# Rotary attention scores on one core: the last eight rows of five GpSimd loads sent, four at a time, to DMA engines 14, 15, 0 and 1

## The chip, the cores and the metric

The kernel runs on one core of a Trainium2 chip. The metric is device time in microseconds (us) of one execution; the lower the better. The core has 16 DMA engines, here numbered 0 to 15, which carry every transfer between HBM and SBUF.

## The reference

Queries and keys are rotated (rotary embedding), and then every query position is multiplied with every key position of the same batch and head. All is float32; nothing follows the scores.

```python
batch, seq, heads, dim = 16, 512, 16, 64
q_rot = concat([q1 * cos - q2 * sin, q1 * sin + q2 * cos], axis=-1)   # q1, q2: halves of dim
k_rot = the same of k
scores = einsum('bshd,bthd->bsht', q_rot, k_rot)                      # 16 x 512 x 16 x 512
```

The two inputs hold 33.6 MB each, the scores 268.4 MB.

## The kernel before

**Tiling.** A batch has 512 positions, four to each of the 128 partitions. A load brings one batch of q or k, 2 MB, as 128 rows of 16 KB (`load`). The work goes in 64 steps `i`, four to a batch. A step multiplies the 16 heads of 128 query positions with all 512 keys (`scores`, L205), copies each pair of heads out of PSUM on ScalarE into a stage tile `st` (L212), and stores that tile, 4 MB, as 128 rows of 32 KB (`store`, L192). There are three stage tiles. In the first four steps (batch 0) sixteen 1 MB stores take the place of these (L215).

**What goes ahead of a step.** VectorE rotates the tiles of q for step i+2 and of k for step i+5 (`rope`, L153, L154, L158). TensorE transposes them (L174) through two PSUM banks; the copies out of those banks are VectorE's for q and ScalarE's for k (L189). Within a step VectorE's queue is written out by hand: products of q, the copy of one bank, sum of q, the copy of the second bank, then products and sum of k. Input tiles have two buffers for each of q and k, so a load waits until TensorE has transposed the batch that held its buffer.

**Queues.** The Sync queue (SP) issues the stores and most loads in the program's order. Its transfers are the queue q1 of the profile; ScalarE's are q10, GpSimd's q0.

**The five GpSimd loads.** `RELIEVED` names five loads, numbered x = 0 to 4: q of batch 6, k of 7, q of 11, k of 12, q of 15. These are not issued by SP but by `load_around`. Its main part moves rows 0 to 119 as two 8 KB pieces each; the eight rows that are left go by another transfer. GpSimd's transfers of n rows, n under 16, are meant to take n engines in a row from a cursor, eight rows of the main part to each of 15 engines. The small loads of `move_cursor(n)`, n rows of 16 bytes into a `scratch` tile that nobody reads, are there to move that cursor by n. Engine 4 (`SLOW`) is the one that the main part leaves out: the cursor stands at 5 when the main part is issued, so it takes 5 to 15 and 0 to 3.

The eight rows that are left go in 2 KB pieces. For even x ScalarE issues them (L102, queue q10), and they go to engines 0 to 7. For odd x GpSimd issues them ahead of the main part, with the cursor at 8, to engines 8 to 15.

Of the kernel before, what the change touches and what calls it, by code (L numbers as in the profile page):

```python
# [10 lines left out]
def kernel(  # L11
# [8 lines left out]
    nc = tc.nc  # L20
# [4 lines left out]
    B, S, H, D = q.shape  # L25
    HD = D // 2
    P = 128
    C = S // P
# [46 lines left out]

    RELIEVED = {("q", 6): 0, ("k", 7): 1, ("q", 11): 2, ("k", 12): 3, ("q", 15): 4}
    SLOW = 4
    scratch = const_pool.tile([P, 96], fp32, name="scratch")
    tiny = [0]  # L80

    def move_cursor(n):

        y = tiny[0]
        tiny[0] += 1
        src = bass.AP(q.tensor, 512 * y, [(512, n), (64, 2), (1, 2)])
        nc.gpsimd.dma_start(scratch[:n, 4 * y : 4 * y + 4].rearrange("p (a b) -> p a b", a=2), src)

    def load_around(which, b, t):

        n, E, SMALL = 120, C * H * D, C * H * D // 8
        x = RELIEVED[which, b]
        d = dram[which][b]

        def pieces(queue, lo, hi, F):
            k = E // F
            src = bass.AP(d.tensor, d.offset + lo * E + E - F, [(E, hi - lo), (-F, k), (1, F)])
            v = t[lo:hi].rearrange("p c e -> p (c e)")  # L100
            dst = bass.AP(v.tensor, v.offset + E - F, [v.ap[0], (-F, k), (1, F)])
            queue.dma_start(dst, src)  # L102

        if x == 0:
            nc.gpsimd.inc_swdge_sem([], [], mode="reset_dge_cursor")
        else:

            move_cursor(16 - SLOW)
        if x % 2:
            move_cursor(8)  # L110
            pieces(nc.gpsimd, n, P, SMALL)
        move_cursor(SLOW + 1)
        pieces(nc.gpsimd, 0, n, E // 2)
        if not x % 2:
            pieces(nc.scalar, n, P, SMALL)

    def load(which, b):

        if b >= B:
            return  # L120
        t = in_pool.tile([P, C, H * D], fp32, tag=which + "_in", name=which + "_sb")
        batches[which, b] = t
        if (which, b) in RELIEVED:
            load_around(which, b, t)
        else:
            nc.sync.dma_start(t.rearrange("p c (h d) -> p c h d", h=H), dram[which][b])
# [199 lines left out]
```

## Time and profile before

| | |
|---|---|
| time, three runs | 792.38, 792.46, 793.31 us; median 792.46 us |
| span of the profiled execution | 789.9 us |
| span short of that median | 2.6 us, which lies around the span |
| TensorE busy | 687.7 us, 87% |
| ScalarE busy | 561.2 us, 71% |
| VectorE busy | 543.8 us, 69% |
| GpSimd busy | 11.9 us, 2% |
| moved by DMA | 336.18 MB, mean 426 GB/s |

The profiled execution has no time of its own beside its span; the three runs were made without a profile. The profile is of one execution: each instruction with start, length and what it waited for, each DMA packet with its queue, start, length and size, and for every transfer the times of the 16 semaphore steps by which the 16 engines report it done. The packets do not carry the number of their engine.

### The profile page before, as it was taken

How to read it: one execution, taken by the hardware profiler on the slowest of the kernel's cores; microseconds unless marked ns; L12 is line 12 of the kernel's file. 1: busy time of each engine (PE TensorE's matmuls, PEld its weight loads, DVE VectorE, ACT ScalarE, POOL GpSimd, SP SyncE). 2: the span in 40 equal slices, each digit the busy share in tenths (PEclk: the TensorE clock that was granted, in tenths of full speed). 3: DMA queues.
4: the chain of work that ended last, by engine and by line, in shares of the span. 5: the costliest groups of instructions: out<-in, count | busy, mean ns of one | idle time of the engine just before them, and what ended most of it. 6: DMA issues, size and time to landing. Idle time of an engine off the chain costs nothing.

```text
span 789.9 us, 7753 instructions
## 1 busy us (share of the span) xinstructions
PE 687.7 (87%) x3072; PEld 297.4 (38%) x3072; DVE 543.8 (69%) x516; ACT 561.2 (71%) x647; POOL 11.9 (2%) x24
## 2 busy tenths in 40 slices
PE   4999998989978989798897988989899798899960
PEld 2444443433423434243343433434334343344420
DVE  7999987667855859566676666767678486587400
ACT  3888886866847868486685865877577586588770
POOL 0000000000001000000000000100000000000000
PEclk9999999999998999899899898999899899899995
DMA  9999999999999999999999999999999999999997
GB/s 353 421 426 440 429 431 435 424 434 440 428 427 429 429 425 406 428 431 436 430 431 434 427 431 427 429 432 429 427 437 422 437 433 433 428 431 436 430 431 339
DMA packets 19100, 336.18 MB, mean 426 GB/s; under 512 B 2376, under 2 KB 3656, under 8 KB 4936
## 3 DMA queue, kind: packets, MB, share of 16 engines
q1 hardware_dynamic: 16288, 324.61, 96.1%
q0 software_dynamic: 1872, 10.10, 3.1%
q10 hardware_dynamic: 904, 0.98, 0.4%
q8 instruction: 24, 0.39, 0.2%
q14 instruction: 12, 0.10, 0.0%
HBM read 67.24 MB, written 268.44 MB: 425 GB/s over the span
## 4 chain that ended last, share of the span: by engine, by line
DMA 46%; PE 39%; DVE 7%; ACT 4%; issue 1%; ACTq 0%
DMA out_dram<-st 45%; PE ps L205 29%; PE bank L174 9%; ACT st L212 4%; DVE part L153 2%; DVE early L154 1%; DVE early L158 1%; DMA early<-in_q_dram 1%; DVE k_sb L158 1%; DVE k_sb L154 1%; DVE kT_t L189 0%; DVE q_sb L154 0%; DVE q_sb L158 0%; ACTq L321 0%; DVE qT_t L189 0%
## 5 line engine op out<-in xcount | busy, mean ns | idle before, releaser
L212 ACT COPY st<-ps 128x1024 f32<-128x1024 f32 x512 | 495.0, 1020 | 193.7 <-DMA out_dram<-st 109.1
L205 PE MATMUL ps<-kT_t,qT_t 64*128 64x512 f32 x2048 | 545.6, 650 | 64.3 <-ACT st L212 64.1
L205 PEld LDWEIGHTS ps<-kT_t,qT_t 64*128 64x128 f32 x2048 | 183.3, 196 | 255.3 <-issue 135.4
L189 DVE COPY qT_t<-bank 128x512 f32<-128x512 f32 x118 | 81.5, 690 | 186.5 <-PE bank L174 186.5
L174 PEld LDWEIGHTS bank<-ident,q_sb 128*128 128x128 f32 x480 | 55.4, 151 | 100.5 <-issue 97.6
L174 PE MATMUL bank<-ident,q_sb 128*128 128x128 f32 x480 | 86.8, 308 | 0.4 <-PE ps L205 0.4
L174 PEld LDWEIGHTS bank<-ident,k_sb 128*128 128x128 f32 x480 | 50.3, 140 | 94.6 <-issue 42.3
L174 PE MATMUL bank<-ident,k_sb 128*128 128x128 f32 x480 | 78.6, 287 | 1.2 <-DVE qT_t L189 1.2
L153 DVE TENSOR_TENSOR part<-k_sb,ss_t 128x1024 f32<-128x1024 f32 x60 | 72.9, 1215 | 9.3 <-DMA k_sb<-in_k_dram 9.2
L189 ACT COPY kT_t<-bank 128x512 f32<-128x512 f32 x122 | 72.4, 598 | 6.9 <-PE bank L174 6.9
L154 DVE TENSOR_TENSOR k_sb<-k_sb,cos_t 128x1024 f32<-128x1024 f32 x60 | 73.5, 1225 | 2.0
L158 DVE TENSOR_TENSOR k_sb<-k_sb,part 128x1024 f32<-128x1024 f32 x60 | 73.5, 1225 | 2.1
L154 DVE TENSOR_TENSOR q_sb<-q_sb,cos_t 128x1024 f32<-128x1024 f32 x60 | 73.5, 1225 | 2.1
L153 DVE TENSOR_TENSOR part<-q_sb,ss_t 128x1024 f32<-128x1024 f32 x60 | 73.5, 1224 | 2.0
L158 DVE TENSOR_TENSOR q_sb<-q_sb,part 128x1024 f32<-128x1024 f32 x60 | 72.9, 1215 | 0.0
L174 PE MATMUL bank<-ident,early 128*128 128x128 f32 x64 | 10.5, 316 | 12.2 <-DVE early L158 9.7
L174 PEld LDWEIGHTS bank<-ident,early 128*128 128x128 f32 x64 | 8.3, 161 | 17.3 <-issue 13.9
L153 DVE TENSOR_TENSOR part<-early,ss_t 128x1024 f32<-128x1024 f32 x8 | 9.8, 1222 | 5.7 <-DMA early<-in_k_dram 4.9
L102 POOL DMA_DIRECT2D q_sb<-in_q_dram x3 | 2.3, 754 | 617.4 <-PE bank L174 617.4
L158 DVE TENSOR_TENSOR early<-early,part 128x512 f32<-128x512 f32 x16 | 10.3, 685 | 0.2
L154 DVE TENSOR_TENSOR early<-early,cos_t 128x1024 f32<-128x1024 f32 x8 | 9.8, 1225 | 0.3
L189 ACT COPY qT_t<-bank 128x512 f32<-128x512 f32 x10 | 5.7, 628 | 3.3 <-PE bank L174 3.3
(12 smaller groups left out, 15.9 us busy)
## 6 DMA issues: line engine op xcount, KB each, us to landing
out_dram<-st SPq DMA_DIRECT2D x60, 4096.0 KB, 25.2
k_sb<-in_k_dram SPq DMA_DIRECT2D x13, 2048.0 KB, 27.7
q_sb<-in_q_dram SPq DMA_DIRECT2D x12, 2048.0 KB, 27.6
out_dram<-st SPq DMA_DIRECT2D x16, 1024.0 KB, 14.5
q_sb<-in_q_dram POOLq DMA_DIRECT2D x3, 1920.0 KB, 29.2
k_sb<-in_k_dram POOLq DMA_DIRECT2D x2, 1920.0 KB, 43.2
early<-in_k_dram SPq DMA_DIRECT2D x1, 1536.0 KB
early<-in_q_dram SPq DMA_DIRECT2D x1, 1536.0 KB, 12.4
```

Of the source, the lines that this page charges most:

```text
L102: queue.dma_start(dst, src)
L153: nc.vector.tensor_tensor(pv, xs, ss, op=mult)
L154: nc.vector.tensor_tensor(xc, xc, cs, op=mult)
L158: nc.vector.tensor_tensor(y, y, z, op=add)
L174: nc.tensor.transpose(bank[:, x, :], src, ident)
L189: copy(out=dst, in_=src)
L205: nc.tensor.matmul(out=po, lhsT=lhs[64 * r : 64 * r + 64, :], rhs=rh, start=True, stop=True)
L212: nc.scalar.copy(out=so, in_=si)
```

## The change

All eight left rows of all five loads are now issued by GpSimd, ahead of the main part, as two transfers of four rows each, in 8 KB pieces like the main part's. Before each of the two the cursor is moved to 14, so that each puts one row on the engines 14, 15, 0 and 1. ScalarE's three transfers are gone, and the order of the rows is the same for all x. GpSimd issues 30 transfers where it issued 18: 15 cursor moves in place of 11, 15 transfers of rows in place of 7.

```diff
-    SLOW = 4
+    SLOW, AHEAD = 4, 14
...
-        n, E, SMALL = 120, C * H * D, C * H * D // 8
+        n, E = 120, C * H * D
...
         if x == 0:
             nc.gpsimd.inc_swdge_sem([], [], mode="reset_dge_cursor")
-        else:
-
-            move_cursor(16 - SLOW)
-        if x % 2:
-            move_cursor(8)
-            pieces(nc.gpsimd, n, P, SMALL)
-        move_cursor(SLOW + 1)
+        move_cursor(AHEAD if x == 0 else (AHEAD - SLOW) % 16)
+        pieces(nc.gpsimd, n, n + 4, E // 2)
+        move_cursor(12)
+        pieces(nc.gpsimd, n + 4, P, E // 2)
+        move_cursor((SLOW + 1 - AHEAD - 4) % 16)
         pieces(nc.gpsimd, 0, n, E // 2)
-        if not x % 2:
-            pieces(nc.scalar, n, P, SMALL)
```

GpSimd's order for x = 0 was: cursor 5, main part (and ScalarE's eight rows). It becomes: cursor 14, four rows, cursor 12, four rows, cursor 3, main part. For odd x it was: cursor 12, cursor 8, eight rows, cursor 5, main part; for x = 2 and 4 cursor 12, cursor 5, main part. For x = 1 to 4 it becomes: cursor 10, four rows, cursor 12, four rows, cursor 3, main part. TensorE, VectorE and SP have the same instructions in the same order as before.

## The prediction

> **What bounds the kernel now.** I read the page's queue rows first.
>
> ```profile
> q1 hardware_dynamic: 16288, 324.61, 96.1%
> q0 software_dynamic: 1872, 10.10, 3.1%
> q10 hardware_dynamic: 904, 0.98, 0.4%
> q8 instruction: 24, 0.39, 0.2%
> ```
>
> The last column adds up to 99.8% of 16 engines' span: the DMA engines never rest, and no compute engine is over 87%. So time is packet time, and what a change of engines can bring lies in how evenly the 16 finish. The DMA row of the last 15 us (40 slices of 0.37 us) shows that they don't:
>
> ```profile
> DMA  9299489969969948948896696692492226000000
> ```
>
> The busy share fades from about 782.7 us on. The 16 semaphore steps of the last store, in the trace, give each engine's end: 782.71, 782.87, 783.55 and 783.64 us for four leaders, twelve from 785.8 on, the last 789.02. Their mean is 786.56, so perfect balance would gain 2.46 us (0.31%), and no more.
>
> Next, the waits on transfers and the issues:
>
> ```profile
> ACT st L212 <- DMA out_dram<-st: 109.1, 41, 6.2
> DVE part L153 <- DMA k_sb<-in_k_dram: 9.2, 2, 4.6
> ...
> out_dram<-st SPq DMA_DIRECT2D x60, 4096.0 KB, 25.2
> q_sb<-in_q_dram POOLq DMA_DIRECT2D x3, 1920.0 KB, 29.2
> k_sb<-in_k_dram POOLq DMA_DIRECT2D x2, 1920.0 KB, 43.2
> ```
>
> ScalarE waits for stage tiles, as it should when DMA is the bound; a store takes 25.2 us to land though 8 packets of 1.21 us are 9.7 us of work, so more than one store is queued. But the two k loads of GpSimd are already late: VectorE waits 4.6 us for each.
>
> **Who the leaders are.** A packet starts 3 to 4 ns before the one ahead of it on its engine ends, so the packets can be chained into engines. Around 500 us the leaders' chains on q0 differ as the small transfers do: used engines show a 16-byte packet for a cursor row, others an 8-byte filler. Two leaders show cursor 12 used (4 to 15), cursor 8 unused, four 4 KB packets of the eight rows, cursor 5 unused: they lie in 8 to 15. Two show 12 unused, 8 used, no rows, 5 used: they lie in 0 to 3. One chain with 32 KB packets of 1.24 to 1.26 us, where the others take 1.213, carries no main part: engine 4. None of the 16 KB instruction packets (q8) after 500 us falls on a leader. If the leaders stand side by side, only 14, 15, 0, 1 has two in each group. The packets do not show it outright.
>
> **The change, part by part.** An 8 KB packet takes 309 ns, 0.305 net of the overlap, so a row as two of them 0.61 us. A row as ScalarE's eight 2 KB packets (84 ns) was 0.64 us, and as GpSimd's four of 4 KB (159 ns) 0.62.
> - Engines 14, 15: ten rows more, two less: 6.1 − 1.2 = +4.9 us.
> - Engines 0, 1: ten more, three less: 6.1 − 1.9 = +4.2 us.
> - Engines 2 to 7, the relieved 4 among them: three less, −1.9 us.
> - Engines 8 to 13: two less, −1.2 us.
> - Cursor rows, fillers and semaphore packets: counted transfer by transfer some 28 more packets per engine, at 6 ns net: +0.2 us everywhere.
>
> If 14, 15 are the leaders without ScalarE's rows, they end at 782.87 + 4.9 = 787.8; 0, 1 at 783.64 + 4.2 = 787.8; the last other engine at 789.02 − 1.2 = 787.8 (it is one of 8 to 13; engine 4, 0.1 us ahead of it, gains 1.9). With the small packets 788.0 in place of 789.02: **−1.0 us**. From the span to the run: 792.46 − 1.0 = 791.4 us. ScalarE's three issues (0.72 to 1.29 us) vanish from a queue that waits 109.1 us anyway: nothing; if that cover were gone, 2.7 us at most. GpSimd's twelve more issues at 0.56 to 0.76 us: nothing, its engine is idle for 617 us before three of them; uncovered, they would delay a main part by 2.4 us.
>
> **The wait that the change adds.** On an engine with both queues filled, q0 and q1 take turns packet by packet: in the main part of x = 0 the 8 KB packets of one engine come 1.5 us apart (1.213 + 0.309), and each small transfer needs two turns (its semaphore steps come 2.4 us after those of the one ahead). By the Trainium skill ("DMA: Bandwidth & Descriptors", Queues, rings and completion order) an engine round-robins its queue rows by packet; the trace agrees with the 1.5 us.
>
> From the start of x = 0 to the end of x = 1 there were 17 + 2 + 2 + 5 + 2 + 17 = 45 turns (main, cursors 12 and 8, eight rows, cursor 5, main). There will be 3 + 2 + 3 + 2 + 17 = 27 and 2 + 3 + 2 + 3 + 2 + 17 = 29: 56. The q load has 10 turns more, at 1.2 us: it lands at 257.7 + 12 = 270, and VectorE took it at 268.65, a wait of some 1 us. The k load has 11 more: 293.05 + 13 = 306.
>
> ```profile
> 287.84 0.69 DVE L189 COPY qT_t<-bank 128x512 f32<-128x512 f32 x1 [3.66 <-PE bank L174]
> 293.17 1.22 DVE L153 TENSOR_TENSOR part<-k_sb,ss_t 128x1024 f32<-128x1024 f32 x1 [4.63 <-DMA k_sb<-in_k_dram]
> ...
> 299.35 0.68 DVE L189 COPY qT_t<-bank 128x512 f32<-128x512 f32 x1
> ```
>
> VectorE's wait grows from 4.6 to about 18 us, and the copy of 299.35 stands behind it. TensorE's transposes at 300.70 need that bank, the scores behind them stop, and the stores issued at 305.15, 315.17 and 332.75 us move to about 318, 328 and 338 (10 us a step). They are hidden by what is queued: the leaders finished the transfer ahead of each at 321.7, 331.4 and 341.1. At x = 3 it is closer: stores of 550.84, 560.86 and 577.93 move to 563, 573 and 583, against 564.7, 574.4 and 584.1; since the first packets come about 2 us after an issue (2.3 us to the first semaphore step of a 64 KB load at the start), the leaders may idle up to 1 us. The other twelve come 2 to 6 us later, and the leaders by then carry some 3.6 us more than before, so I take **0**; bounds: 0 and, at 6 us more lateness at both places, +6 us. A gain from it is excluded, as no packet disappears. The q loads (x = 2 and x = 4) land at about 514 and 709 us, and VectorE takes those tiles at 514.1 and 709.2: nothing, or 1 to 2 us of VectorE alone.
>
> **The rivals.**
> - *The leaders are not all 14, 15, 0, 1.* Then an engine that ends between 785.8 and 789.0 gets 4.2 to 4.9 us more, and the end moves to between 790 and 793.9: 793.4 to 797.4 us. For it: the class is shown, not the number. Against it: the two classes, and the instruction packets that pass the leaders by. It decides once one of the four ends after 784.1. The Trainium skill (same page, Latency and other measured facts) says that engines 7 and 15 are usually the slower ones, which speaks against loading 15; by that rule 15 would end last and the time be 797.4. In this trace the one engine with longer packets is 4, and nothing shows 15 slow. I give 15% in all.
> - *The late k loads reach DMA.* Price: if VectorE's wait passes about 22 us instead of 18, all engines go idle by the excess, at x = 1 and x = 3. 1 to 3 us at both: 793.4 to 797.4. For it: margins of 1 to 4 us against turns counted to some 3 us. Against it: as q1 runs dry, q0's turns get shorter. 17%.
> - *The cursor does not go where its arithmetic says* (a four-row transfer spreads in another way): the eight rows fall on other engines and the main part may hit engine 4, 8 rows or 4.9 us each time. 797 us or more. The 8- and 120-row transfers did land as reckoned, so 4%.
> - *Balance comes out better,* because the last engines of this execution were held up by chance (packets of up to 2.02 us occur): near 790.3 us, 6%.
>
> **The numbers.** The forecast has 58%, its own range 790.6 to 792.3. The low end of the range (790.4) takes in most of the better balance, the high end (796.0) most of the late k loads and half of the wrong engines. A change of 0.2% (1.6 us) is about what can be told from none, the three runs being 0.93 us apart. Faster than 790.9: 6% and 12% out of the forecast's own spread. Slower than 794.0: 15 + 13 + 4 = 32%. The rest, 50%, is within.
>
> **What would show it.** Right: the last store's 16 steps lie within some 5 us, none before 783.5, the last about 1 us earlier than now; VectorE's two waits for k loads are 14 to 20 us; GpSimd's k loads land 55 us after issue; q10 loses 216 packets; busy DMA stays at 99.8%. Wrong: a last step 4 us behind the next (a misplaced engine), slices of DMA under 9 around 320 or 565 us (the stall came through), or long gaps in a 4-row transfer's steps.

## The result, and the profile after

| | before | after |
|---|---|---|
| time, six runs of each taken together | 792.88 us median (791.47 to 794.41) | 798.25 us median (797.46 to 799.33) |
| ratio, 95% interval | | 1.0066 (1.0054 to 1.0079) |
| span of the profiled execution | 789.9 us | 796.7 us |
| semaphore steps of the last store: mean of 16, last | 786.56, 789.02 us | 789.56, 795.57 us |

The change made the kernel 5.2 us slower (0.66% of 792.5 us; 4.3 to 6.3). In what follows every effect in us is a measured ratio less one, times 792.5 us, unless a median is named.

The queue rows and the issues of the page after:

```profile
q1 hardware_dynamic: 16288, 324.61, 95.5%
q0 software_dynamic: 2320, 10.49, 3.2%
q10 hardware_dynamic: 688, 0.59, 0.2%
...
out_dram<-st SPq DMA_DIRECT2D x60, 4096.0 KB, 24.6
...
q_sb<-in_q_dram POOLq DMA_DIRECT2D x3, 1920.0 KB, 37.5
k_sb<-in_k_dram POOLq DMA_DIRECT2D x2, 1920.0 KB, 55.2
```

q1's 16288 packets and 324.61 MB are unchanged, q10 has lost its 216 packets, and the k loads of GpSimd take 55.2 us to land where they took 43.2. The three shares add up to 98.9% where they were 99.6: the engines have more unused time, and the DMA row of the last 15 us, in 40 slices, shows where it lies:

```profile
DMA  9969899894998886644222022222020020000000
```

A slice at 2 is some three of the 16 engines. The fade now drags on for nearly 9 us: the 16 steps run from 787.08 to 790.22 for thirteen engines, and then come 792.66, 793.52 and 795.57. (Before, the last five lay within 0.75 us.) So two things happened. The last engine is 6.0 us behind the mean in place of 2.5, and the mean itself is 3.0 us later. Summed over the packets of the two profiles and divided by 16 engines, 2.4 of these 3.0 us are packet time: 1.3 in the 16 KB packets of SP's loads, 0.6 in the 32 KB packets of the stores, and 0.55 in GpSimd's and ScalarE's queues together. The other 0.6 us is time without a packet, about half of it in the first 20 us.

The late k load is plain to see. First VectorE's waits, then the first of them on its timeline (start, length, line, in brackets the idle time before), then windows of the whole core, whose last two columns are the share of the 16 DMA engines and GB/s:

```profile
DVE qT_t L185 <- PE bank L170: 163.5, 107, 7.4
DVE part L149 <- DMA k_sb<-in_k_dram: 36.9, 2, 20.8
```

```profile
306.25 1.23 DVE L149 TENSOR_TENSOR part<-k_sb,ss_t 128x1024 f32<-128x1024 f32 x1 [20.81 <-DMA k_sb<-in_k_dram]
```

```profile
300.00:320.00 20.00, 7.30 (x24) 3.17 (x22) 13.48 (x13) 4.41 (x6) 0.00 (x0) 0.66 0.99 409
320.00:340.00 20.00, 20.00 (x98) 8.85 (x96) 17.08 (x17) 17.35 (x21) 0.00 (x0) 1.00 1.01 434
340.00:360.00 20.00, 20.00 (x98) 8.85 (x96) 17.06 (x17) 17.34 (x21) 0.00 (x0) 1.00 0.99 398
560.00:580.00 20.00, 20.00 (x96) 8.99 (x96) 17.87 (x18) 16.52 (x19) 0.00 (x0) 0.96 1.01 432
```

TensorE works 7.3 of the 20 us from 300 on, and the DMA engines stay full through it. But from 340 to 360 us, behind the stall, the same share moves 398 GB/s and not 434: the packets took longer there (16 KB packets 723 ns on average, 32 KB packets 1248; in the kernel before, in the same 20 us, 613 and 1218). Such a stretch is nothing new by itself: the kernel before has one from 300 to 320 us, with 390 GB/s and 16 KB packets of 712 ns. These two readings, the placement at the end and the longer packets, are what the experiments are about.

### The profile page after: what moved, and what is told of

Read it like the earlier page. It is cut to its first block, busy times and chain, and to the rows that moved or that the text cites. A ratio compares the mean times of both kernels' runs of the same rounds, so it can differ in the third digit from the quotient of the medians.

```text
span 796.7 us, 7769 instructions
## 1 busy us (share of the span) xinstructions
PE 682.1 (86%) x3072; PEld 296.2 (37%) x3072; DVE 544.2 (68%) x516; ACT 561.5 (70%) x647; POOL 19.0 (2%) x36
## 3 DMA queue, kind: packets, MB, share of 16 engines
q1 hardware_dynamic: 16288, 324.61, 95.5%
## 4 chain that ended last, share of the span: by engine, by line
DMA 40%; PE 40%; DVE 7%; another core or an unknown queue 5%; ACT 4%; issue 1%; ACTq 0%; DVEq 0%
DMA out_dram<-st 40%; PE ps L201 30%; PE bank L170 10%; ACT st L208 4%; DVE part L149 2%; DVE k_sb L154 1%; DVE k_sb L150 1%; DVE early L154 1%; DVE q_sb L150 1%; DVE early L150 1%; DMA early<-in_k_dram 0%; DVE kT_t L185 0%; DVE qT_t L185 0%; DVE q_sb L154 0%
## 5 line engine op out<-in xcount | busy, mean ns | idle before, releaser
L201 PE MATMUL ps<-kT_t,qT_t 64*128 64x512 f32 x2048 | 539.9, 644 | 56.3 <-ACT st L208 56.0
L170 PE MATMUL bank<-ident,k_sb 128*128 128x128 f32 x480 | 80.4, 291 | 21.8 <-DVE qT_t L185 21.7
L170 PE MATMUL bank<-ident,q_sb 128*128 128x128 f32 x480 | 84.9, 303 | 0.6 <-PE ps L201 0.6
L102 POOL DMA_DIRECT2D q_sb<-in_q_dram x9 | 5.9, 653 | 622.3 <-PE bank L170 622.3
L87 POOL DMA_DIRECT2D scratch<-in_q_dram x15 | 8.8, 585 | 0.3 <-issue 0.3
## 6 DMA issues: line engine op xcount, KB each, us to landing
k_sb<-in_k_dram POOLq DMA_DIRECT2D x2, 1920.0 KB, 55.2
```

The costliest lines, as they stand in the source:

```text
L170: nc.tensor.transpose(bank[:, x, :], src, ident)
L201: nc.tensor.matmul(out=po, lhsT=lhs[64 * r : 64 * r + 64, :], rhs=rh, start=True, stop=True)
```

## The experiments

As in the prediction, a leader is an engine that ends its part of the last store well ahead of the rest. P is the theory that the rows were placed on the wrong engines, that is, that 14, 15, 0 and 1 are not all leaders. L is its rival, that the late loads and the further transfers of GpSimd set the end, whatever the engines.

### Which engine is which

The packets do not carry their engine's number. Marks give it: after the last main part, cursor moves of two rows each put 16-byte packets on two engines at a time, and an 8-byte filler on the fourteen others. Followed backward from the last store, each engine's chain of packets then shows its pair. First the kernel before, then the changed kernel with the same marks.

```diff
             pieces(nc.scalar, n, P, SMALL)
+        if x == 4:
+            for _ in range(8):
+                move_cursor(2)
```

> The kernel before, with eight two-row cursor loads added behind the last GpSimd load, so that the packet records tell which pair of engines (4/5, 6/7, ... 2/3) each chain is. Theory P (placement: the four leaders are not all 14, 15, 0, 1): of the pairs 14/15 and 0/1 at least two engines are not among the first four to finish the last store, but end 3 us or more behind the first; the time stays 792 to 794 us. Theory L (lateness: the leaders are 14, 15, 0, 1, and the cost comes from the later k loads): both pairs are the leaders, all four within 1 us of the first.

> The changed kernel with the same eight marks. Theory P: the three engines that end 5.6, 6.4 and 8.5 us behind the first belong to the pairs 14/15 and 0/1, and the time stays 797 to 800 us. Theory L: the late three are other engines, held up while the k loads were late.

The kernel before with marks took 793.89 us in one run (792.56 without), the changed one 798.1. A third run had the pairs shifted by one (`move_cursor(3)` ahead of the eight), to split the pairs of the first:

> The kernel before, with the eight two-row marks shifted by one engine (7/8, 9/10, 11/12, 13/14, 15/0, 1/2, 3/4, 5/6). With the first marked run each leader has one number. If the leaders are a regular set such as every second engine, they come out as such; if they differ from execution to execution, the pairs of the two runs contradict each other. Of 14, 15, 0 and 1 two are leaders in either case, two end 2 us or more behind them. Time 792 to 794 us.

It took 792.81 us. The ends of the last packets (a semaphore step comes some 0.4 us later), by pair:

| pair | before, marked | | pair | before, marked, shifted |
|---|---|---|---|---|
| 14/15 | 783.86, 787.06 | | 15/0 | 782.33, 783.02 |
| 0/1 | 783.92, 786.40 | | 1/2 | 782.87 and one of the late |
| 2/3 | 784.17, 787.23 | | 7/8 | 783.17, 784.04 |
| 8/9 | 784.24, 787.76 | | others | 785.86 to 789.38 |
| 6/7 | 784.36, 787.43 | | | |
| 12/13 | 787.53, 788.65 | | | |
| 4/5 | 787.46, 790.34 | | | |

Both of 15/0 lead in the second, and one of 14/15 and one of 0/1 in the first: so 15 and 0 lead, and 14 and 1 do not. In the same way 8 and 7 lead, and 2. (7 is a fifth leader, which the profile of before does not have.) The changed kernel with marks confirms it from the other side: its four last engines are 14/15 at 792.75 and 794.38 and 0/1 at 790.13 and 792.50 us, and all the others end from 786.88 to 789.68. By the prediction's own arithmetic, from the marked ends of before, 14 would be at 787.06 + 4.9 = 792.0 and 1 at 786.40 + 4.2 = 790.6. If the later one of each pair is the one that was late before, they are at 794.4 and 792.5: 2.4 and 1.9 us more than the arithmetic gives. Engine 0 (788.1 by the arithmetic, 790.1) shows as much, and 15 (788.8, 792.75 at the earliest) 4 us. So the rows put 14 and 1 last, but they are not all that moved the ends. The engines without added rows show it too: 2, 7 and 8 carry fewer rows than before and should have ended from 782.3 to 783.0 us, but no engine of the pairs 2/3, 6/7 and 8/9 ends before 787.3. The early engines have lost their lead, loaded or not.

### Other engines for the same rows

One constant moves the four rows, and nothing else:

```diff
-    SLOW, AHEAD = 4, 14
+    SLOW, AHEAD = 4, 15     # first run
+    SLOW, AHEAD = 4, 10     # second run
```

> The changed kernel with the four rows on engines 15, 0, 1, 2 in place of 14, 15, 0, 1 (one number; transfers, turns and waits are the same). Theory P, the marks read rightly (15, 0 and 2 end early in the kernel before, 14 and 1 do not): the last engine of the changed kernel, 14, is relieved of 6.1 us; 15 and 1, at 1.6 to 1.9 us ahead of it, are then the last, with 2: about 1.6 us faster than the changed kernel, 796.7 us. Theory L, that the late loads and the extra transfers set the end whatever the engines: 798.2 us as before the edit. The prediction's reading (14, 15, 0, 1 the leaders): slower than the changed kernel, near 801 us.

> The changed kernel with the four rows on engines 10 to 13, none of which ends early in the kernel before (786.6 to 788.7 us in the marked run). Theory P: the last of them ends 1.6 us later than engine 14 would (788.65 against 787.06 us in the marked run): about 799.8 us. Theory L: 798.2 us. The prediction's reading (four leaders robbed of nothing, four late engines loaded): near 799 to 801 us too, so this run tells only L from the rest.

With 15, 0, 1, 2 the ratio to before is 1.0043 (1.0029 to 1.0056), median 795.81 us; with 10 to 13 it is 1.0090 (1.0076 to 1.0104), 799.38 us. The changed kernel's 1.0066 lies between. Between these two runs nothing but one number differs, and it is worth 3.7 us; the late loads and the further transfers are the same in both, so L cannot explain it. The prediction's reading, by which leaving 14 loses, has the wrong sign. The last 15 us of the second, with four engines far behind:

```profile
DMA  9449289889962962804242242062062002000000
```

Its last store's steps come at 794.88, 795.01, 795.46 and 796.25 us, the one before at 790.86: the four that were loaded. Then the rows spread as before over engines 0 to 7 (even x) and 8 to 15 (odd x), with the changed kernel's number of transfers:

```diff
-        move_cursor(AHEAD if x == 0 else (AHEAD - SLOW) % 16)
+        at = 8 if x % 2 else 0
+        move_cursor(16 if x == 0 else (at - SLOW) % 16)
         pieces(nc.gpsimd, n, n + 4, E // 2)
-        move_cursor(12)
+        move_cursor(16)
         pieces(nc.gpsimd, n + 4, P, E // 2)
-        move_cursor((SLOW + 1 - AHEAD - 4) % 16)
+        move_cursor((SLOW + 1 - at - 8) % 16)
```

> The changed kernel's transfers, packets and turns (two four-row transfers of 8 KB pieces and three cursor loads ahead of each main part), but the rows on the engines that the kernel before gave them: 0 to 7 for even x, 8 to 15 for odd x. The k loads stay as late as in the changed kernel (VectorE waits 15 to 21 us for each). Theory P: the time goes back to that of the kernel before, 792.5 to 794.5 us, with the spread of the last store's 16 steps near 6 us. Theory L: it stays at 797 to 799 us.

Ratio 1.0022 (1.0013 to 1.0032), median 794.51 us. VectorE waits as long as in the changed kernel, and the fade is short again but for one engine, whose step comes at 792.49 us, 2.0 us behind the next. The first step comes at 786.29 us, so the early engines have lost their lead here as well:

```profile
DVE part L150 <- DMA k_sb<-in_k_dram: 40.5, 2, 21.0
```

```profile
DMA  9988999699899999969869664242020020000000
```

So placement is worth 5.2 − 1.7 = 3.5 us, and 1.7 us are left with every row on the engines of before.

### The other 1.7 us

**Late k loads alone**: five cursor moves by 16 ahead of the odd loads, all else as before.

```diff
         if x % 2:
+            for _ in range(5):
+                move_cursor(16)
             move_cursor(8)
```

> The kernel before, with five 16-row cursor loads more ahead of each of the two GpSimd k loads: ten turns more on queue q0, no row moved to another engine. VectorE's waits for the two k loads grow from 4.6 to 15 to 20 us. If lateness is what the spread kernel (1.9 us over the kernel before) still paid, this one pays it too: 794 to 795 us. If that came from the four-row transfers or from the rows that ScalarE no longer moves, it stays within 0.8 us of the kernel before.

Ratio 1.0011 (1.0002 to 1.0020): 0.9 us, with 0.2 to 1.6 possible. VectorE's wait is nearly that of the changed kernel:

```profile
DVE part L155 <- DMA k_sb<-in_k_dram: 36.7, 2, 18.4
```

**Its opposite**, the wait of before cut to half by larger pieces (`E // 2` in place of `SMALL` for odd x):

> The kernel before, with the eight rows of the two k loads in 8 KB pieces in place of 2 KB: two turns less on q0 ahead of each k load, same engines, same bytes. VectorE's waits for them fall from 4.6 to about 2 us. Theory: that wait is hidden in the kernel before, so the time is the same within 0.5 us; if lateness costs from the first microsecond, it is 0.3 to 0.8 us faster.

Ratio 0.9997 (0.9988 to 1.0006): no difference, with each wait at 2 us in place of 4.6. The 2.6 us that went away were hidden.

```profile
DVE part L153 <- DMA k_sb<-in_k_dram: 4.0, 2, 2.1
```

**The even loads alone.** Only the three q loads' rows go by GpSimd, once four at a time to 15, 0, 1, 2 and once to 0 to 7, the engines that ScalarE's transfers use; odd x stays as before. (The edit is shown shortened: the branch for odd x, which the `else` belongs to, is as before.)

```diff
+        else:
+            move_cursor(at if x == 0 else (at - SLOW) % 16)    # at = 15; at = 0: 16, 12
+            pieces(nc.gpsimd, n, n + 4, E // 2)
+            move_cursor(12)                                    # at = 0: 16
+            pieces(nc.gpsimd, n + 4, P, E // 2)
+            move_cursor((SLOW + 1 - at - 4) % 16)              # at = 0: 13
...
-        if not x % 2:
-            pieces(nc.scalar, n, P, SMALL)
```

> The kernel before with the rows of the even loads alone (the three q loads) by GpSimd to 15, 0, 1, 2, four at a time; the odd loads as before, so the k loads are late only by what the q loads give on. Theory P: engine 4, the last at 790.3 us in the marked run, loses three rows (-1.9), 1 comes to 788.3, 15 to 787.5, and the last is 13 at 788.7: 1.7 us faster, 790.8 us, less what the added transfers cost (up to 1.2 us): 790.8 to 792.0 us. Theory L: 794 us or more, like the spread rows.

> The kernel before with the rows of the even loads alone by GpSimd, four at a time, to the same engines 0 to 7 as ScalarE's transfers took; the odd loads as before. No engine carries other bytes than before, and the k loads' own turns are as before. If the 1.9 us that the spread rows lost are the lateness of the k loads (0.8 us, shown alone) and the taking of q's rows from ScalarE's queue into GpSimd's (the rest): about 1.1 us slower, 793.6 us. If the k loads' lateness is all of it and the rest belongs to longer stalls: no change, 792.5 us.

1.0028 (1.0017 to 1.0038) and 1.0037 (1.0025 to 1.0049). The first was to gain and lost 2.2 us. The second, in which no engine gets other rows, lost 2.9 us, more than was expected of it. In both GpSimd's q loads hand their delay on to the k loads behind them, though those have only their own old turns:

```profile
q_sb<-in_q_dram POOLq DMA_DIRECT2D x3, 1920.0 KB, 37.4
k_sb<-in_k_dram POOLq DMA_DIRECT2D x2, 1920.0 KB, 53.4
```

(the issue rows of the second). With one transfer of eight rows in place of two of four the loss is smaller:

```diff
+            move_cursor(12 if x else 16)
+            pieces(nc.gpsimd, n, P, E // 2)
+            move_cursor(SLOW + 9)
```

> As the run with the even rows by GpSimd spread over 0 to 7 (2.5 us slower than before), but with one transfer of eight rows in place of two of four: the same rows on the same engines and queue, one transfer and one cursor move fewer per even load, so some five turns fewer and the k loads about 6 us less late. Theory R, that taking the rows from ScalarE's queue to GpSimd's costs as such: 794.4 us or more, as there. Theory T, that each further transfer of GpSimd costs (its cursor moves, its turns): it adds one move to each of two loads only; 792.5 to 793.2 us.

1.0014 (1.0005 to 1.0023), 1.1 us, with waits for k of 11.9 us at most. Its median, 793.6 us, is between what the two theories gave (794.4 or more if moving the rows to GpSimd's queue costs as such, 792.5 to 793.2 if each further transfer costs), nearer to the second.

**The added transfers as such**, first with fifteen cursor moves:

```diff
-    scratch = const_pool.tile([P, 96], fp32, name="scratch")
+    scratch = const_pool.tile([P, 112], fp32, name="scratch")
...
+        if not x % 2:
+            for _ in range(5):
+                move_cursor(16)
         move_cursor(SLOW + 1)
```

> The kernel before with five more cursor moves by 16 ahead of the main part of each even load (the three q loads): the q loads land ten turns, some 12 us, later, and push the k loads behind them back, as in the run with the even rows by GpSimd; but ScalarE still brings the eight rows, no engine carries other rows, and the added packets are 15 x 3 of 7 to 17 ns per engine, 0.2 to 0.4 us. If the 2.5 us that the even rows by GpSimd cost are the lateness of q and k: 794.5 to 795 us. If they are the moving of the rows from ScalarE's queue to GpSimd's: only what late k loads cost alone (0.8 us), 793.1 us. The prediction's account (late loads are hidden, small packets cost 6 ns): 792.5 to 792.7 us.

1.0050 (1.0038 to 1.0063). The run did not do what it was made for: a cursor move waits for no buffer, so GpSimd issued these long ahead of the load (in the first microseconds, and right behind the k loads, near 260 and 510 us), and nothing was late (VectorE's longest wait for k 4.0 us). Yet it lost 4.0 us. Two runs took the moves apart:

> The kernel before with ten of the fifteen added cursor moves of the earlier run (those of x = 2 and x = 4, which run right behind a k load near 300 and 545 us), without the five of x = 0, which run in the first microseconds. If each added transfer costs alike (4.0 us for fifteen): 2.7 us, 795.2 us. If the five of the start cost the most (packets of the 16 KB loads from 60 to 240 us were longer in that run): 792.7 to 793.3 us, like the ten moves ahead of the odd loads (0.8 us).

> The kernel before with only the five added cursor moves of x = 0, which run in the first microseconds. If each added transfer costs alike: 1.3 us, 793.8 us. If the start is what matters: 3 us or more, 795.5 us or later.

1.0051 (1.0038 to 1.0065) with ten of the moves, 1.0036 (1.0024 to 1.0049) with the other five: neither by number nor by place. The three share something else. Fifteen more moves need more columns of `scratch`, and all three runs have the larger tile, 112 columns of 4 bytes in place of 96, which puts the tiles that are laid out behind it 64 bytes further on in their partitions. (That follows from the kernel's text; the profile shows no addresses.) Three runs separated the tile from the moves:

> The kernel before with the scratch tile of 112 in place of 96 columns and nothing else: every later tile lies 64 bytes further on in its partition. The three runs with added moves that also had this larger tile were 2.9 to 4.1 us slower, all with longer 16 KB load packets from 60 to 240 us, where their moves do not run. If the addresses make the packets longer: about 2.9 us slower, 795.4 us, with the excess of q1's packets at 7 us in place of 4.4. If it was the moves: 792.5 us.

> The kernel before with a scratch tile of 128 columns: later tiles lie 128 bytes further on than in the kernel before, at a multiple of 512 bytes. If what counts is whether a tile starts at a multiple of 128 bytes (96 columns do so too, 112 do not): 792.5 us. If a multiple of 512 is better still: up to 1 us less, as the 16 KB loads after 300 us have some 1 us of excess now. If any shift costs: 795 us.

> The ten added cursor moves in mid-run once more, with the scratch tile of 96 columns as in the kernel before, so that no address differs. If added transfers cost by their number: 795 to 796 us. If the addresses cost 2.9 us of the 4.0 that the run with 112 columns lost: about 793.3 us, near the 0.8 us of the ten moves ahead of the odd loads.

The tile alone, with no other edit, costs 3.6 us at 112 columns (1.0045, 1.0029 to 1.0062) and 2.4 us at 128 (1.0030, 1.0019 to 1.0041). The ten moves alone cost nothing that can be told: 1.0002 (0.9994 to 1.0011). The windows from 40 to 120 us, where none of the moves runs, of the run with 112 columns and of the run with ten moves and 96:

```profile
40.00:120.00 80.00, 76.74 (x375) 34.51 (x374) 74.46 (x73) 67.83 (x80) 0.00 (x0) 1.00 1.01 427
```

```profile
40.00:120.00 80.00, 76.62 (x375) 34.52 (x374) 74.46 (x73) 67.86 (x80) 0.00 (x0) 1.00 1.01 432
```

Equally full engines move 427 in place of 432 GB/s. Most of the loss lies in the 16 KB packets of SP's loads: their mean over the execution is 619.5 ns before, 631.3 at 112, 629.4 at 128 and 621.8 with ten moves at 96. An engine carries 200 of them, so 1 ns is 0.2 us of it: 2.4 of the 3.6 us at 112 columns, 2.0 of the 2.4 at 128.

The changed kernel has the tile of before, so the larger tile is no cause of its loss. But its 16 KB packets are longer as well: 626.2 ns, or 1.3 us an engine, against 623.3 with the spread rows, 625.2 with the even rows spread by fours, and 619.6 both with the late k loads alone and with the one transfer of eight. In the changed kernel 0.8 of the 1.3 us come in one burst behind the first stall (the 398 GB/s above) and 0.3 around the end of the second, from 540 to 560 us. The profiles of kernels with the tile of before and without rows by fours on GpSimd's queue have 618.7 to 621.8 ns, late k loads and added transfers among them; the seven with rows by fours have 621.0 (on 15, 0, 1, 2) to 626.2. So neither lateness nor added transfers make the packets longer by themselves, and the rows by fours on GpSimd's queue go with longer packets in most profiles. Why, no run here shows. The early engines' lost lead, too, goes with the slower kernels, with the larger tile as with the rows by fours (first step at 786.37 us with 112 columns); what comes first is open.

**An attempt to gain**: ScalarE's eight rows as two transfers of four, which keeps GpSimd's queue as it was.

```diff
-            pieces(nc.scalar, n, P, SMALL)
+            pieces(nc.scalar, n, n + 4, SMALL)
+            pieces(nc.scalar, n + 4, P, SMALL)
```

> The kernel before with ScalarE's eight rows of the three q loads as two transfers of four, still by ScalarE in 2 KB pieces: nothing is added to GpSimd's queue, no load is later. Theory P, with four rows going to engines 0 to 3 twice (not shown so far): 0 to 3 get three rows more (+1.9 us), 4 to 7 three less; engine 4 comes from 790.3 to 788.4, 1 from 786.4 to 788.3, 3 from 787.2 at most to 789.1, 13 stays at 788.7 (times of the marked run): the last 1.2 us earlier, 791.1 us. If four rows are spread over all 16 engines by their pieces: engine 4 loses half of its rows, 0.6 to 1 us earlier, 791.5 us. Theory L (lateness and transfers by GpSimd alone count): 792.3 us, no change.

1.0005 (0.9996 to 1.0014), no gain. At x = 4 none of ScalarE's packets lies on engine 4's chain of packets any more, and four other engines have two rows each, so 4 was relieved. It ended at 788.54 us all the same, where the profile of before has it at 788.55. The gain forecast for 4 was 1.9 us, and the engine's end differs by nearly as much from execution to execution: in the marked run of the kernel before, with the same rows, it came at 790.34 us. So one profile cannot tell whether the relief moved it; the eleven runs' time shows no gain. No version tried beats the kernel before.

## Why the prediction was wrong

**The step that failed** is the identity of the leaders: "If the leaders stand side by side, only 14, 15, 0, 1 has two in each group. The packets do not show it outright." The class was right, two in 8 to 15 and two in 0 to 3: 15 and 8, 0 and 2. That all four stand side by side was assumed, and is false. Two of the four engines that got ten rows more were late ones, 14 and 1, and the leaders 8 and 2 got none. This is the first rival. It decides, as the prediction put it, "once one of the four ends after 784.1": 14 and 1 end at 787.06 and 786.40. The moved constant (1.0043, 1.0066, 1.0090) and the spread rows (1.0022) show it: 3.5 of 5.2 us. That two of the four were leaders all the same was luck: nothing in the packets told 15 and 0 from 14 and 1.

**A term that was too small**: the further transfers and moved rows were put at "+0.2 us everywhere", and cost 1.7 us with the engines left as they were. That, and not placement alone, put the time (798.25 us) even above that rival's 797.4. The small packets themselves were sized rightly: they take 0.25 us more on an engine in the profile of after. What was left out is that other packets grow longer: the 16 KB packets by 1.3 us, the 32 KB packets by 0.6, and GpSimd's 8 KB pieces by 0.45 (315.5 ns for 309.9, most of it from 695 to 700 us, where they take up to 621 ns). Late k loads alone cost 0.9 us, which the prediction took at 0, within its bounds of 0 and 6. The cause of the rest is open, and the parts do not add up: the even rows alone, on the engines of before, lost 2.9 us.

**The late loads** were predicted to within 3 us. 56 turns gave 306 us for the k load of x = 1, and it landed at 306.06; the q load landed at 268.40 (270 predicted), VectorE waited 20.8 and 16.1 us (18), and the three stores behind it were issued at 320.4, 330.4 and 340.4 us (318, 328, 338), 564, 574 and 584 at x = 3 (563, 573, 583). The DMA engines' idle time from 320 to 360 us is 0.2 us: the stall was covered, as predicted, and the second rival (late loads reach DMA) is not what happened. The Trainium skill ("DMA: Bandwidth & Descriptors", Queues, rings and completion order) has an engine round-robin its queue rows by packet; the count of 11 turns more for 13 us agrees with it.

**The cursor** goes where its arithmetic says, also with transfers of four rows: in the marked run the last four are the four loaded engines. That was the third rival, and it is out. The better balance, the fourth, did not come.

**Engine 15.** The Trainium skill (same page, Latency and other measured facts) says that engines 7 and 15 are usually slower. Here both are among the first to finish in the marked runs of the kernel before (783.86 us for 15, 784.36 for 7, the late engines from 786.4 on), so the measurement differs. In the changed kernel the marks do not tell 15 from 14, which end at 792.75 and 794.38 us. With the rows on 15, 0, 1 and 2 the kernel is 1.8 us faster, so 14 cost more than 2 does; what 15 cost is not shown apart.

**The signs that were named**: the 55 us to landing and the 216 packets came as said; of the two waits, put at 14 to 20 us, 16.1 us lies inside and 20.8 just above. The busy share of DMA fell from 99.8 to 99.1%. "The last store's 16 steps lie within some 5 us" did not come: 8.5 us, with the last three 2.4 us and more behind the other thirteen. The sign named for a misplaced engine was a last step 4 us behind the next. Here the last is 2.1 us behind the next, because a group was late and not one engine, and this too was in the first view of the result.

## What to carry to other kernels

When the gain hangs on which engine a chain of packets is, mark the engines first: a few tiny transfers at the end, in a kernel that changes nothing else, settle it before anything is moved. A class that fits a neat pattern (four in a row) is not an identity; price the change for each member of the class. And when an experiment enlarges a tile to make room, run the enlarged tile alone: here that edit cost 3.6 of the 4.0 us that the experiment showed.

## What the runs showed of the hardware

- A tile that nobody reads, made 64 or 128 bytes longer in each partition, made the whole kernel 3.6 or 2.4 us slower, most of it through the length of 16 KB load packets (619.5 ns to 631.3 and 629.4). The median packet stays at 611 ns; the length that one packet in a hundred exceeds goes from 988 to 1171 and 1141 ns. That the places of the tiles behind it are the cause is likely, but the profile shows no addresses.
- The engines that finish first in the marked runs of the kernel before are 15, 0, 2, 7 and 8, which are not one row of neighbours. Engine 4 is slow by its packets: it took 89.6 us for the last nine stores where undisturbed engines took 87.1, in the profile of before and in the run with ScalarE's rows by fours alike.
- A small transfer of GpSimd delays what follows on its queue, and puts packets on the engines that it does not use as well. Beside a full SP queue five of them ahead of a k load made VectorE start on it at 304.2 us in place of 293.2: 2.2 us each, about two turns of 1.2 us. But ten of them that nothing waits for cost 0.2 us (−0.5 to 0.9).
